# Where the norms, residuals and operand sums of a two-layer mixer block keep their intermediates: SBUF on two engines, or unused PSUM banks on VectorE alone

## The chip, the cores and the metric

The kernel runs on one core of a Trainium2 chip. The metric is device time in microseconds (us), from the start to the end of one execution. Five engines work beside each other and are kept in step by semaphores: TensorE (PE; PEld is its weight load), VectorE (DVE), ScalarE (ACT), GpSimd (POOL) and SyncE (SP), which here issues nearly all DMAs. Tensors lie in SBUF or in one of eight PSUM banks of 128 partitions x 512 float32 numbers; TensorE writes to PSUM.

## The reference, cut to what matters

Two layers over 256 context tokens and 1024 latent tokens of 1024 channels, in float32. Each layer normalises, projects, runs three recurrent mixers (retention, GLA, RWKV-7), projects back with `w_out`, adds a normed residual, normalises again, runs a SwiGLU of 2816 hidden channels, and adds a second normed residual:

```
def _rmsnorm(x, g, eps=1e-6):
    y = x * rsqrt(mean(x * x, axis=-1) + eps)
    return y * g

u = (rmsnorm(x) * (1 + sc1) + sh1) @ w_in
...
x = x + gt1 * rmsnorm(y @ w_out, norm_mix_post)
h = rmsnorm(x, norm_ffn_pre) * (1 + sc2) + sh2
f = (silu(h @ w_gate) * (h @ w_up)) @ w_down
x = x + gt2 * rmsnorm(f, norm_ffn_post)
```

The context tokens go through the same in the first layer alone.

## The kernel before, in words

Activations are held channel-major: 128 partitions by 8 channel tiles (`KT`, index kt) by the tokens of a block. There are three blocks: block 0 is the context (256 tokens), blocks 1 and 2 are 512 latent tokens each. A matmul keeps float32 accuracy by splitting both operands into a rounded high part and a low part (high on ACT by a cast, low by a subtraction), and making three products (`mm3`, `dense_cm`). Weights are split as they stream in: in `slot` (line 1459) ACT writes `shi` and POOL, for most slots, `slo` (L1464); in `weights` ACT writes `whi` and POOL `wlo` (L447).

Four helpers stand around the changed lines.

- `rstd` (L349) sums the squares of the 8 channel tiles over partitions by a matmul with ones into a bank of tag n (`pn`), and makes 1/sqrt(mean + eps) of it with Ln and Exp on ACT, in an SBUF tile `nrs`. With `pe=True` there is one ones-matmul for each kt. With `pe=False` ACT squares into `nacc`, `nacc2` and `nsq`, DVE adds the even kt (L370), POOL the odd ones (L372), DVE joins the two sums (L373), and one matmul follows.
- `resid` (L401) computes f = f * rstd * gain + x: the product into an SBUF tile `nv` of two buffers (L411: kt 2 and 5 on POOL, the other six on DVE), then a scalar_tensor_tensor on DVE (L412); the result goes to DRAM in two halves.
- `norm_here` (L392) multiplies in place (L398: kt 2 and 5 on POOL) and applies scale and shift on ACT.
- `split_norm` (L378) multiplies into `nv` (L386, same sharing), applies scale and shift on ACT, casts to the high part `xh` on DVE (L388), and subtracts to the low part `xl` (L390, odd kt on POOL, even kt on DVE).

`operands` (L1494) makes the sums and splits of a Strassen-like product for the hidden layer: s1 = a21 + a22, s2 = s1 - a11, s3 = a11 - a21 (L1510 to L1512) in the SBUF tiles `nsq`, `nacc` and `nacc2` of one buffer each, a21 = a12 - s2 (L1513), then a cast on ACT and a subtraction for S2, S3, S1 and 12 (L1503; S1 on POOL, the others on DVE).

The stretches of the program in which these run, in order:

- the start: `split_norm` of all three blocks, with `pe=True`, while the first `w_in` weights arrive; PSUM holds 3 banks of tag d (`pd`), 3 of tag m (`pm`), 2 of tag n. After it `rwkv_in` projects from `xh`, `xl` into `pd`.
- the FFN of the first layer (`ffn`, L1623), with 4 banks d, 3 banks m, 1 bank n: residual and norm of block 0 behind the last `w_out` column; then `hidden_plain` of block 0 (11 steps) on PE in banks d, with residual and norm of blocks 1 and 2 and `operands` issued between its steps; then `hidden` with the Strassen products. In this up part nothing uses the m banks.
- its down projection: a first pass over the weights for block 1, a second one for blocks 0 and 2. Products go through the m banks and DVE adds each to `facc` (L1741); the d banks are unused. Residual and `split_norm` of block 1 (`pe=False`) run under the second pass; those of blocks 0 and 2 (`pe=True`) follow it, and behind them the next layer's `rwkv_in`, for which both PSUM pools are closed and opened anew.
- the FFN of the second layer: the same without the context, residual, norm and `operands` of block 2 beside `hidden` of block 1 for three steps; at the very end the residual of block 2, which writes the output.

Instructions are put in order for each engine by a scheduler that simulates the time line; within an engine they run in that order. SP issues DMAs in the same way.

Of the kernel before, what the change touches and what calls it, by code (L numbers as in the profile page):

```python
# [50 lines left out]
NV = 2  # L51
# [120 lines left out]
class Kern:  # L172
# [176 lines left out]
    def rstd(self, x, b, dst, pe=False):  # L349


        nc = self.nc
        n = BLK[b][1]
        ps = self.pn()
        if pe:
            for kt in range(KT):
                sq = self.t(self.N, [128, 512], ("nsq", "nacc", "nacc2")[kt % 3], bufs=1)[:, :n]
                self.act(sq, x[:, kt, :], AF.Square)
                self.mm(ps[:, :n], self.ones, sq, start=kt == 0, stop=kt == KT - 1)
        else:  # L360
            acc = self.t(self.N, [128, 512], "nacc", bufs=1)[:, :n]
            acc2 = self.t(self.N, [128, 512], "nacc2", bufs=1)[:, :n]
            for kt in range(KT):
                if kt < 2:
                    self.act(acc2 if kt else acc, x[:, kt, :], AF.Square)
                    continue
                sq = self.t(self.N, [128, 512], "nsq", bufs=1)[:, :n]
                self.act(sq, x[:, kt, :], AF.Square)
                if kt % 2 == 0:
                    nc.vector.tensor_tensor(acc, acc, sq, op=ALU.add)  # L370
                else:
                    nc.gpsimd.tensor_tensor(acc2, acc2, sq, op=ALU.add)  # L372
            nc.vector.tensor_tensor(acc, acc, acc2, op=ALU.add)  # L373
            self.mm(ps[:, :n], self.ones, acc)
        self.act(dst, ps[:, :n], AF.Ln, bias="e6", scale=1.0 / D)
        self.act(dst, dst, AF.Exp, scale=-0.5)

    def split_norm(self, x, b, A, B, s, xh, xl, pe=False):  # L378

        nc = self.nc  # L380
        n = BLK[b][1]
        rs = self.t(self.N, [128, 512], "nrs", bufs=1)[:, :n]
        self.rstd(x, b, rs, pe)
        for kt in range(KT):
            v = self.t(self.N, [128, 512], "nv", bufs=NV)[:, :n]
            (nc.gpsimd if kt % 3 == 2 else nc.vector).tensor_tensor(v, x[:, kt, :], rs, op=ALU.mult)  # L386
            self.act(v, v, AF.Identity, bias=B[:, kt, s:s + 1], scale=A[:, kt, s:s + 1])
            nc.vector.tensor_copy(xh[:, kt, :], v)  # L388
            e = nc.gpsimd if kt % 2 else nc.vector
            e.tensor_tensor(xl[:, kt, :], v, xh[:, kt, :].bitcast(F32), op=ALU.subtract)  # L390

    def norm_here(self, x, b, A, B, s):  # L392

        n = BLK[b][1]
        rs = self.t(self.N, [128, 512], "nrs", bufs=1)[:, :n]
        self.rstd(x, b, rs)
        for kt in range(KT):
            (self.nc.gpsimd if kt % 3 == 2 else self.nc.vector).tensor_tensor(x[:, kt, :], x[:, kt, :], rs, op=ALU.mult)  # L398
            self.act(x[:, kt, :], x[:, kt, :], AF.Identity, bias=B[:, kt, s:s + 1], scale=A[:, kt, s:s + 1])

    def resid(self, f, b, gp, s, xsrc, xdst, pe=False, px=None):  # L401
# [5 lines left out]
        rs = self.t(self.N, [128, 512], "nrs", bufs=1)[:, :n]  # L407
        self.rstd(f, b, rs, pe)
# [1085 lines left out]
    def operands(self, xc, p, T):  # L1494
# [12 lines left out]
        for kt in range(4):  # L1507
            a11, a12, a21, a22 = T[0][:, kt, :], T[0][:, kt + 4, :], T[1][:, kt, :], T[1][:, kt + 4, :]
            s1, s2, s3 = (self.t(self.N, [128, 512], x, bufs=1)[:, :n] for x in ("nsq", "nacc", "nacc2"))
# [4 lines left out]
            for i, (name, src) in enumerate((("S2", s2), ("S3", s3), ("S1", s1), ("12", a12))):  # L1514
                split(name, kt, src, g if i % 3 == 2 else v)
# [452 lines left out]
```

## Time and profile before, and how to read it

| | |
|---|---|
| median of 3 runs | 4202.64 us (4200.39 to 4202.81) |
| the profiled execution | 4200.48 us, span 4198.7 us |
| PE busy | 3837.7 us (91%), 30414 instructions |
| PEld busy | 3170.7 us (76%) |
| DVE busy | 2668.9 us (64%), 4510 instructions |
| ACT busy | 1740.9 us (41%) |
| POOL busy | 1678.4 us (40%) |
| mean granted clock of PE | 0.951 |

The profile is one execution. A row of the windows view gives, for a stretch, its length and the busy time of each engine (with the number of instructions), the granted clock of TensorE as a share of full speed (1.00 is 2.4 GHz), the share of the DMA engines' time and the bytes moved. A row of the lines view gives a line of the program, engine, operation, output and inputs, shape, count, then busy us in total and mean ns of one, then the idle time of the engine before them and who ended it. A row of the waits view reads "engine line waited for: us in total, times, longest".

### The profile page before, as it was taken

The numbers are of one execution on the slowest core, as the hardware profiler recorded it, in microseconds if no ns is written. First come the engines' busy times: TensorE is split into PE (matmuls) and PEld (weight loads), VectorE is DVE, ScalarE is ACT, GpSimd is POOL, SyncE is SP. The second block draws the span as 40 slices with busy tenths as digits, with TensorE's granted clock in tenths as the row PEclk, the third lists the DMA queues.
The fourth block names the chain that finished last, engine by engine and source line by source line (L and its number), as shares of the span: only waits on it lengthen the run. The fifth ranks groups of instructions, "written<-read, shape, count | busy, mean of one in ns | idle before, by whom it ended". The sixth has DMA issues, their size and how long they took to land. (4 is left out here: it accounts for less than half of the span.)

```text
span 4198.7 us, 78278 instructions
## 1 busy us (share of the span) xinstructions
PE 3837.7 (91%) x30414; PEld 3170.7 (76%) x30414; DVE 2668.9 (64%) x4510; ACT 1740.9 (41%) x3490; POOL 1678.4 (40%) x1775
## 2 busy tenths in 40 slices
PE   6998999789988899999997997999889887999998
PEld 3777887776667888887785676888856667999876
DVE  3465657667647766665765464667667578556665
ACT  4443334244435644433423443343244355344432
POOL 3146630333338832224533245740433454222453
PEclk8998999999999899999998997999989889999999
DMA  5587545666433422225331387655673132212542
GB/s 174 137 229 192 142 130 151 186 188 192 141 122 126 151 103 80 81 90 192 132 106 55 86 232 198 137 140 141 206 225 117 57 126 89 86 71 95 185 163 95
DMA packets 624771, 582.55 MB, mean 139 GB/s; under 512 B 315276, under 2 KB 517264, under 8 KB 607504
## 3 DMA queue, kind: packets, MB, share of 16 engines
q1 hardware_dynamic: 624112, 576.50, 45.0%
q8 instruction: 240, 3.93, 0.4%
q0 software_dynamic: 288, 1.05, 0.1%
q14 instruction: 131, 1.07, 0.1%
HBM read 431.14 MB, written 146.28 MB: 138 GB/s over the span
## 5 line engine op out<-in xcount | busy, mean ns | idle before, releaser
L1464 POOL TENSOR_TENSOR slo<-raw,shi 128x512 fp32r<-128x512 f32 x467 | 690.9, 1494 | 964.6 <-ACT shi L1463 894.0
L1463 ACT CAST shi<-raw 128x512 fp32r<-128x512 f32 x478 | 293.0, 619 | 492.7 <-PE pd L246 196.3
L1741 DVE TENSOR_TENSOR f<-pm,f 128x512 f32<-128x512 f32 (+1 forms) x400 | 252.1, 635 | 186.7 <-PE pm L246 184.5
L246 PE MATMUL pm<-hh,shi 128*128 128x512 f32 (+1 forms) x880 | 333.8, 380 | 19.5 <-DVE f L1741 10.2
L246 PE MATMUL pm<-hl,shi 128*128 128x512 f32 (+1 forms) x880 | 327.2, 372 | 0.0
L246 PE MATMUL pm<-hh,slo 128*128 128x512 f32 (+1 forms) x880 | 326.3, 371 | 0.0
L447 POOL TENSOR_TENSOR wlo<-wraw,whi 128x512 fp32r<-128x512 f32 x120 | 166.8, 1399 | 386.7 <-ACT whi L446 376.1
L246 PE MATMUL pd<-whi,xh 128*128 128x256 f32 x1072 | 315.6, 296 | 1.9 <-DVE st L451 1.9
L246 PE MATMUL pd<-wlo,xh 128*128 128x256 f32 x1072 | 314.5, 294 | 1.8 <-POOL wlo L447 1.8
L246 PE MATMUL pd<-whi,xl 128*128 128x256 f32 x1072 | 315.0, 294 | 0.0
L246 PE MATMUL pd<-xl,whi 128*128 128x512 f32 (+1 forms) x720 | 278.1, 387 | 12.5 <-POOL xl L390 8.6
L246 PE MATMUL pd<-xh,whi 128*128 128x512 f32 (+1 forms) x720 | 276.9, 385 | 11.6 <-DVE xh L388 11.5
L246 PE MATMUL pd<-xh,wlo 128*128 128x512 f32 (+1 forms) x720 | 271.5, 377 | 1.1 <-POOL wlo L447 1.1
L1463 ACT CAST shi<-tw 128x512 fp32r<-128x512 f32 x200 | 123.6, 619 | 305.3 <-PE pd L246 231.9
L246 PEld LDWEIGHTS pd<-wlo,xh 128*128 128x128 f32 x1072 | 211.5, 197 | 10.3 <-issue 6.0
L246 PEld LDWEIGHTS pd<-whi,xh 128*128 128x128 f32 x1072 | 210.9, 197 | 9.2 <-DVE st L451 2.5
L246 PEld LDWEIGHTS pd<-whi,xl 128*128 128x128 f32 x1072 | 211.2, 197 | 5.8 <-issue 3.7
L246 PEld LDWEIGHTS pm<-hh,shi 128*128 128x128 f32 x880 | 167.5, 191 | 58.0 <-DVE f L1741 18.3
L246 PEld LDWEIGHTS pm<-hl,shi 128*128 128x128 f32 x880 | 167.8, 191 | 29.6 <-issue 1.7
L246 PEld LDWEIGHTS pm<-hh,slo 128*128 128x128 f32 x880 | 167.2, 190 | 28.9
L1464 DVE TENSOR_TENSOR slo<-tw,shi 128x512 fp32r<-128x512 f32 x200 | 145.1, 727 | 67.0 <-ACT shi L1463 66.7
L246 PEld LDWEIGHTS pd<-xl,whi 128*128 128x128 f32 x720 | 141.5, 197 | 53.3 <-POOL xl L390 13.5
(395 smaller groups left out, 11218.4 us busy)
## 6 DMA issues: line engine op xcount, KB each, us to landing
raw<-in_wgu SPq DMA_DIRECT2D x72, 1024.0 KB
wmod<-in_w_mod SPq DMA_DIRECT2D x192, 256.0 KB
raw<-in_wd SPq DMA_DIRECT2D x44, 1024.0 KB
wraw<-in_w_in SPq DMA_DIRECT2D x100, 256.0 KB
a<-ops SPq DMA_DIRECT2D x80, 288.0 KB
h<-h SPq DMA_DIRECT2D x44, 512.0 KB
h<-u SPq DMA_DIRECT2D x19, 1024.0 KB
X<-ops SPq DMA_DIRECT2D x36, 480.0 KB
```

The source lines that it names most:

```text
L246: return self.nc.tensor.matmul(out, l, r, start=start, stop=stop, skip_group_check=skip)
L447: nc.gpsimd.tensor_tensor(wl[i][:, :, w], r, wh[i][:, :, w].bitcast(F32), op=ALU.subtract)
L1463: self.nc.scalar.copy(hi, src)
L1464: e.tensor_tensor(lo, src, hi.bitcast(F32), op=ALU.subtract)
L1741: nc.vector.tensor_tensor(facc[b][:, m, :], ps, facc[b][:, m, :], op=ALU.add)
```

## The change

All intermediates of these helpers go to PSUM banks that the stretch doesn't use: `self.tmp` is `pm` (3 banks) at the start and in the up part, `pd` (4 banks) in the down part. `rstd` keeps 1/sqrt in its n bank, in place, and returns it, so the bank is held until the last product that reads it. With `pe=False` all seven sums go to DVE. The products of `resid`, `norm_here` and `split_norm` all go to DVE, with a PSUM output; scale and shift run from PSUM (in `split_norm` to PSUM). The high part of `split_norm` moves from DVE to ACT, and all low parts to DVE. In `operands` s1 to s3 lie in PSUM, S1 moves from POOL to DVE, and 12 from DVE to POOL. The tiles `nrs` and `nv` go away. In the down part `resid` and `split_norm` of blocks 0 and 2 change from `pe=True` to `pe=False`; at the start `pe=True` stays.

```diff
-    def rstd(self, x, b, dst, pe=False):
+    def rstd(self, x, b, pe=False):
...
+        acc = None if pe else self.tmp()[:, :n]
+        for kt in range(KT):
+            sq = self.t(self.N, [128, 512], ("nsq", "nacc", "nacc2")[kt % 3], bufs=1)[:, :n]
+            if not pe and kt == 0:
+                self.act(acc, x[:, kt, :], AF.Square)
+                continue
+            self.act(sq, x[:, kt, :], AF.Square)
+            if pe:
+                if kt == 0:
+                    ps = self.pn()[:, :n]
+                self.mm(ps, self.ones, sq, start=kt == 0, stop=kt == KT - 1)
+            else:
+                nc.vector.tensor_tensor(sq if kt == KT - 1 else acc, acc, sq, op=ALU.add)
+        if not pe:
+            ps = self.pn()[:, :n]
+            self.mm(ps, self.ones, sq)
+        self.act(ps, ps, AF.Ln, bias="e6", scale=1.0 / D)
+        self.act(ps, ps, AF.Exp, scale=-0.5)
+        return ps
...
     def split_norm(self, x, b, A, B, s, xh, xl, pe=False):
...
-            v = self.t(self.N, [128, 512], "nv", bufs=NV)[:, :n]
-            (nc.gpsimd if kt % 3 == 2 else nc.vector).tensor_tensor(v, x[:, kt, :], rs, op=ALU.mult)
+            v = self.tmp()[:, :n]
+            nc.vector.tensor_tensor(v, x[:, kt, :], rs, op=ALU.mult)
             self.act(v, v, AF.Identity, bias=B[:, kt, s:s + 1], scale=A[:, kt, s:s + 1])
-            nc.vector.tensor_copy(xh[:, kt, :], v)
-            e = nc.gpsimd if kt % 2 else nc.vector
-            e.tensor_tensor(xl[:, kt, :], v, xh[:, kt, :].bitcast(F32), op=ALU.subtract)
+            nc.scalar.copy(xh[:, kt, :], v)
+            nc.vector.tensor_tensor(xl[:, kt, :], v, xh[:, kt, :].bitcast(F32), op=ALU.subtract)
...
     def norm_here(self, x, b, A, B, s):
...
-            (self.nc.gpsimd if kt % 3 == 2 else self.nc.vector).tensor_tensor(x[:, kt, :], x[:, kt, :], rs, op=ALU.mult)
-            self.act(x[:, kt, :], x[:, kt, :], AF.Identity, bias=B[:, kt, s:s + 1], scale=A[:, kt, s:s + 1])
+            v = self.tmp()[:, :n]
+            self.nc.vector.tensor_tensor(v, x[:, kt, :], rs, op=ALU.mult)
+            self.act(x[:, kt, :], v, AF.Identity, bias=B[:, kt, s:s + 1], scale=A[:, kt, s:s + 1])
...
     def resid(self, f, b, gp, s, xsrc, xdst, pe=False, px=None):
...
-            v = self.t(self.N, [128, 512], "nv", bufs=NV)[:, :n]
-            (nc.gpsimd if kt % 3 == 2 else nc.vector).tensor_tensor(v, f[:, kt, :], rs, op=ALU.mult)
+            v = self.tmp()[:, :n]
+            nc.vector.tensor_tensor(v, f[:, kt, :], rs, op=ALU.mult)
             nc.vector.scalar_tensor_tensor(f[:, kt, :], v, gp[:, kt, s:s + 1], xo[:, kt, :], op0=ALU.mult, op1=ALU.add)
...
     def operands(self, xc, p, T):
...
-            s1, s2, s3 = (self.t(self.N, [128, 512], x, bufs=1)[:, :n] for x in ("nsq", "nacc", "nacc2"))
+            split("12", kt, a12, g)
+            s1, s2, s3 = (self.tmp()[:, :n] for _ in range(3))
...
-            for i, (name, src) in enumerate((("S2", s2), ("S3", s3), ("S1", s1), ("12", a12))):
-                split(name, kt, src, g if i % 3 == 2 else v)
+            for name, src in (("S2", s2), ("S3", s3), ("S1", s1)):
+                split(name, kt, src, v)
...
     def ffn(self, l, f, gp1, A2, B2, gp2, A1n, B1n):
...
+        self.tmp = self.pm
...
+        self.tmp = self.pd
...
-                self.resid(facc[b], b, gp2, s, self.XD[1], self.out if last else self.XD[0], b != 1)
+                self.resid(facc[b], b, gp2, s, self.XD[1], self.out if last else self.XD[0])
...
-                    self.split_norm(facc[b], b, A1n, B1n, s, nh[b], nl[b], b != 1)
+                    self.split_norm(facc[b], b, A1n, B1n, s, nh[b], nl[b])
...
     def run(self):
...
+        self.tmp = self.pm
```

## Rows read from the trace of the kernel before

**Rows 1.** The windows view: the eight stretches in which the changed helpers run.

```profile
38.00:97.00 59.00, 42.66 (x108) 22.07 (x107) 36.43 (x54) 33.74 (x56) 31.31 (x40) 0.75 0.23 63
1236.00:1255.00 19.00, 1.73 (x7) 0.94 (x6) 9.60 (x20) 7.15 (x17) 9.18 (x10) 0.64 1.04 392
1255.00:1481.00 226.00, 190.95 (x1217) 172.71 (x1216) 165.59 (x154) 136.28 (x249) 186.45 (x128) 0.90 0.42 146
2040.00:2120.00 80.00, 71.77 (x374) 59.01 (x373) 66.92 (x95) 34.05 (x57) 39.92 (x28) 0.96 0.32 110
2238.00:2306.00 68.00, 45.53 (x127) 25.86 (x126) 39.12 (x65) 32.84 (x58) 27.73 (x37) 0.80 0.29 85
3434.00:3541.00 107.00, 80.57 (x553) 75.39 (x553) 103.05 (x149) 59.72 (x112) 52.02 (x33) 0.90 0.26 94
4060.00:4090.00 30.00, 27.87 (x116) 21.20 (x115) 27.65 (x36) 10.24 (x15) 18.89 (x12) 1.00 0.49 173
4177.00:4199.00 22.00, 3.40 (x8) 1.14 (x6) 11.70 (x15) 1.95 (x3) 3.28 (x2) 0.65 0.26 96
```

**Rows 2.** Single lines: count, then shortest, median and longest duration in ns.

```profile
L1741 DVE TENSOR_TENSOR f<-pm,f x400: 408/691/693, 1926.6 to 4177.0; 128x512 f32<-128x512 f32 x108, 128x256 f32<-128x256 f32 x26
L412 DVE SCALAR_TENSOR_TENSOR f<-nv,gain,xl x80: 472/742/1786, 1243.3 to 4192.1; 128x512 f32<-128x512 f32 x64, 128x256 f32<-128x256 f32 x16
L398 DVE TENSOR_TENSOR f<-f,nrs x30: 411/1472/1784, 1264.0 to 3506.3; 128x512 f32<-128x512 f32 x24, 128x256 f32<-128x256 f32 x6
L1464 POOL TENSOR_TENSOR slo<-raw,shi x467: 1255/1297/3213, 925.0 to 4163.6; 128x512 fp32r<-128x512 f32 x156
```

**Rows 3.** The time line of DVE near 4070 us: start, length, times.

```profile
4070.40 1.27 DVE L1741 TENSOR_TENSOR f<-pm,f 128x512 f32<-128x512 f32 x2
```

**Rows 4.** The lines view of DVE and POOL, 1255 to 1481 us.

```profile
L412 DVE SCALAR_TENSOR_TENSOR f<-nv,gain,xl 128x512 f32<-128x512 f32 x16 | 21.4, 1359 | 0.1
L398 DVE TENSOR_TENSOR f<-f,nrs 128x512 f32<-128x512 f32 x12 | 19.5, 1690 | 0.1
L372 POOL TENSOR_TENSOR nacc<-nacc,nsq 128x512 f32<-128x512 f32 x12 | 19.0, 1587 | 4.8 <-ACT nsq L239 4.8
```

**Rows 5.** The waits of PE, 1255 to 1481 us.

```profile
PE pd L246 <- DVE u L1618: 13.3, 3, 5.9
PE pd L246 <- POOL slo L1464: 9.0, 10, 3.0
```

**Rows 6.** The lines view of DVE and POOL, 3434 to 3541 us.

```profile
L1464 DVE TENSOR_TENSOR slo<-tw,shi 128x512 fp32r<-128x512 f32 x23 | 20.6, 910 | 0.1
L412 DVE SCALAR_TENSOR_TENSOR f<-nv,gain,xl 128x512 f32<-128x512 f32 x8 | 9.8, 1236 | 0.0
L1503 POOL TENSOR_TENSOR S1l<-nsq,S1h 128x256 fp32r<-128x256 f32 x4 | 9.0, 2252 | 7.7 <-ACT S1h L1502 7.7
```

**Rows 7.** The waits of PE, 2040 to 2120 us.

```profile
PE pm L246 <- DVE f L1741: 8.2, 11, 2.0
```

**Rows 8.** The lines view of ACT, whole span.

```profile
L239 ACT ACTIVATE nv<-nv,modT,gain 128x512 f32<-128x512 f32 x32 | 25.4, 811 | 35.0 <-DVE nv L386 30.7 <-POOL nv L386 4.2
L1463 ACT CAST shi<-raw 128x512 fp32r<-128x512 f32 x478 | 293.0, 619 | 492.7 <-PE pd L246 196.3 <-PE pm L246 130.2 <-issue 120.3
```

**Rows 9.** The time line of DVE at the start: the last `split_norm`, first and last of 17 pieces.

```profile
76.41 1.69 DVE L386 TENSOR_TENSOR nv<-f,nrs 128x512 f32<-128x512 f32 x2 [0.81 <-ACT nrs L239]
...
92.90 0.47 DVE L388 CAST xh<-nv 128x512 fp32r<-128x512 f32 x1 [0.94 <-ACT nv L239]
```

**Rows 10.** The windows view of PE's instructions on tile pd alone, before `rwkv_in` runs freely.

```profile
2238.00:2286.00 48.00, 10.61 (x48) 0.89 0.36 104
```

**Rows 11.** The time lines of PE and DVE in the last 22 us.

```profile
4176.80 1.88 PE L246 MATMUL pn<-nacc,ones 128*128 128x512 f32 x4
...
4181.81 1.29 DVE L411 TENSOR_TENSOR nv<-f,nrs 128x512 f32<-128x512 f32 x2 [4.12 <-ACT nrs L239]
...
4191.49 1.40 DVE L412 SCALAR_TENSOR_TENSOR f<-nv,gain,xl 128x512 f32<-128x512 f32 x2
```

More of the change, by code (lines that the diff above doesn't have):

```diff
@@ L50 @@
 C2 = 1
-NV = 2
 PA = 7
@@ L346, in mod_gain @@
         return o
-    def rstd(self, x, b, dst, pe=False):
+    def rstd(self, x, b, pe=False):
         nc = self.nc
         n = BLK[b][1]
[L354 to L376, printed above, removed]
+        acc = None if pe else self.tmp()[:, :n]
[17 more added lines that the diff above has]
+        return ps
     def split_norm(self, x, b, A, B, s, xh, xl, pe=False):
@@ L381, in split_norm @@
         n = BLK[b][1]
-        rs = self.t(self.N, [128, 512], "nrs", bufs=1)[:, :n]
-        self.rstd(x, b, rs, pe)
+        rs = self.rstd(x, b, pe)
         for kt in range(KT):
-            v = self.t(self.N, [128, 512], "nv", bufs=NV)[:, :n]
-            (nc.gpsimd if kt % 3 == 2 else nc.vector).tensor_tensor(v, x[:, kt, :], rs, op=ALU.mult)
+            v = self.tmp()[:, :n]
+            nc.vector.tensor_tensor(v, x[:, kt, :], rs, op=ALU.mult)
             self.act(v, v, AF.Identity, bias=B[:, kt, s:s + 1], scale=A[:, kt, s:s + 1])
-            nc.vector.tensor_copy(xh[:, kt, :], v)
-            e = nc.gpsimd if kt % 2 else nc.vector
-            e.tensor_tensor(xl[:, kt, :], v, xh[:, kt, :].bitcast(F32), op=ALU.subtract)
+            nc.scalar.copy(xh[:, kt, :], v)
+            nc.vector.tensor_tensor(xl[:, kt, :], v, xh[:, kt, :].bitcast(F32), op=ALU.subtract)
     def norm_here(self, x, b, A, B, s):
         n = BLK[b][1]
-        rs = self.t(self.N, [128, 512], "nrs", bufs=1)[:, :n]
-        self.rstd(x, b, rs)
+        rs = self.rstd(x, b)
         for kt in range(KT):
-            (self.nc.gpsimd if kt % 3 == 2 else self.nc.vector).tensor_tensor(x[:, kt, :], x[:, kt, :], rs, op=ALU.mult)
-            self.act(x[:, kt, :], x[:, kt, :], AF.Identity, bias=B[:, kt, s:s + 1], scale=A[:, kt, s:s + 1])
+            v = self.tmp()[:, :n]
+            self.nc.vector.tensor_tensor(v, x[:, kt, :], rs, op=ALU.mult)
+            self.act(x[:, kt, :], v, AF.Identity, bias=B[:, kt, s:s + 1], scale=A[:, kt, s:s + 1])
     def resid(self, f, b, gp, s, xsrc, xdst, pe=False, px=None):
@@ L406, in resid @@
         self.dma(xo, xsrc[:, :, t0:t0 + n])
-        rs = self.t(self.N, [128, 512], "nrs", bufs=1)[:, :n]
-        self.rstd(f, b, rs, pe)
+        rs = self.rstd(f, b, pe)
         for kt in range(KT):
-            v = self.t(self.N, [128, 512], "nv", bufs=NV)[:, :n]
-            (nc.gpsimd if kt % 3 == 2 else nc.vector).tensor_tensor(v, f[:, kt, :], rs, op=ALU.mult)
+            v = self.tmp()[:, :n]
+            nc.vector.tensor_tensor(v, f[:, kt, :], rs, op=ALU.mult)
             nc.vector.scalar_tensor_tensor(f[:, kt, :], v, gp[:, kt, s:s + 1], xo[:, kt, :], op0=ALU.mult, op1=ALU.add)
```

## The prediction, made before the changed kernel was run

> **What bounds the kernel now.** I read the page first: PE is busy for 91% of the span, so a step off another engine is worth only what it gives back to PE. Then I cut out the eight stretches in which the changed helpers run, with the windows view [rows 1]. Together they are 611 us long, and PE is busy for 464 of them: 147 us idle, and a granted clock between 0.64 and 1.00 where the kernel's mean is 0.951. Everything the change can win is there. They differ in what fills them: from 1255 to 1481 us POOL works for 186 of 226 us and DVE for 166; from 3434 to 3541 us DVE works for 103 of 107; at the start and from 2238 to 2306 us no engine is full, and a chain from engine to engine sets the pace.
>
> Third, single lines. A DVE addition of a PSUM bank to an SBUF tile (L1741) has a median of 0.691 us and a longest of 0.693 in 400 instances, though POOL splits weights beside it. The same size with all tensors in SBUF starts from the same length and stretches to 1.79 us (L412), and for L398 the median is 1.47 us. POOL's weight split stretches too, from 1.26 to 3.21 us [rows 2]. So in this trace DVE and POOL hold each other up when both read SBUF for two inputs, and a DVE instruction with one input in PSUM is out of it. The changed instructions are nearly all of the held-up kind, and they become the other kind.
>
> **Price of an instruction after the change.** Two L1741 in a row take 1.27 us [rows 3], 0.64 each; I take 0.62 for 512 columns in a full queue and 0.35 for 256. No row shows DVE writing to PSUM. The nearest rows read PSUM and write SBUF [rows 2], and I take their price; from below I allow 0.58, since nothing excludes a small gain, from above 0.72, a tenth of a us more. For ACT I take 0.81 for scale and shift and 0.62 for a cast [rows 8], as from SBUF. The Trainium skill, page "ScalarE: Activation LUTs", in the walk through an activation, says that an ACT result in PSUM is quicker than one in SBUF; no row shows it, and by it the two stretches in which ACT sets the pace would end slightly earlier still.
>
> **The sum, stretch by stretch** (negative is time saved).
>
> *The start, 38 to 97 us.* The last `split_norm` takes from 76.41 to 93.4 us, 17 us [rows 9], with two `nv` buffers going round DVE, POOL and ACT. After: 16 DVE instructions of 0.62 are 10 us, ACT's 8 x (0.81 + 0.62) are 11.4, and three banks keep them overlapped, so some 13 us: 4 saved in each of the two wide blocks. Against it, ACT gets 8 casts of 0.4 and 16 of 0.62 more, 13 us on top of its 33.7 in 59 [rows 1]. I take -7, between -12 (59 less ACT's 47) and +2.
>
> *Behind `w_out`, 1236 to 1255 us.* PE idles 17 of 19 us [rows 1] while the first two rstd are made in a chain. A POOL sum of each stands in one queue with weight splits of at least 1.26 us [rows 2]; on DVE it doesn't. The DMA is full there (share 1.04 [rows 1]), so what follows may be late anyway: -3, from -5 to 0.
>
> *`hidden_plain` of block 0, 1255 to 1481 us.* DVE: the 16 L412 fall from 21.4 to 9.9 us; the 12 wide L398 take 19.5 [rows 4], and their 16 successors take 9.9. The other products and sums go the same way, less the four products and twelve sums that arrive from POOL: altogether about 45 us less on DVE. POOL loses 12 sums (19.0 us [rows 4]), 8 wide products and two narrow ones, and the four S1, gains four 12, and its 88 weight splits no longer stretch: about 54 us less. PE's idle time is 35 us, of which the waits for L1618, which stands in DVE's queue, and for POOL's `slo` are 13.3 and 9.0 [rows 5]; and the clock of 0.90 costs 22 us more. I give back two thirds of those 22 us of waits and some of the rest, -18 in all, and 8 of the 22 us of clock: -26, from -45 to -10.
>
> *Block 1 under the second down pass, 2040 to 2120 us.* PE waits 8.2 us for L1741, in 11 waits [rows 7], behind norm instructions in DVE's queue. DVE's part in the norm shrinks by about 9 us of 67, casts and stretching included: -5, from -8 to 0. From 4060 to 4090 us, the residual alone, PE idles 2.1 us [rows 1]: -1.
>
> *Between the layers, 2238 to 2306 us.* Here I put gains against losses. Two `split_norm` shorten as at the start: about -3 (narrow) and -4.5 (wide). Some six narrow ones-matmuls leave the stream of products, at half or less of the 0.94 us that a wide one takes [rows 11]: -2. But the seven sums of each norm, and the four products that POOL did, now stand in DVE's chain: +4.5. And there is a new wait: the d banks, free before, are now `tmp`, and `rwkv_in` writes to d banks. In the trace PE does 10.6 us of that projection before 2286 us, while the last block is still being normed [rows 10]. That work will wait until the last products have left the banks. It is queued in front of everything PE does next; half of it still overlaps the last `split_norm`: +5. Net 0, from -9 to +9.
>
> *`hidden` of block 1 beside block 2, 3434 to 3541 us.* DVE is full, so each us taken from it counts. L412 falls from 9.8 to 5.0 us; the products save 2; the sums cost 2 more; splits from PSUM save 2; the others balance: -8. POOL's 52 us lose some 23, the four S1 of 2.25 us each among them [rows 6], so that what stays in SBUF on DVE is held up less (the 23 `slo` at 0.910 us lie 0.3 above their unhindered length): -7. Together -15, from -26 (all of PE's idle time) to -5.
>
> *The end, 4177 to 4199 us.* The last four ones-matmuls run one after the other behind the last product (1.88 us for the first two, in four records [rows 11]) and leave PE's stream: -3.5 together, one DVE sum more included. Then 16 DVE instructions without POOL take 10.4 us, where they and POOL's two took from 4181.8 to 4192.9, 11.1 us [rows 11]: -0.5. I take -4, from -5 to 0.
>
> The sum is -7 - 3 - 26 - 5 - 1 + 0 - 15 - 4 = -61. The profiled execution took 4200.5 us by itself, so 4139.5; the median of the runs is 2.2 us higher, and I forecast **4141 us**.
>
> **The rivals.**
>
> *Only the edges go* (4180 us). The 226 us from 1255 on hold 22 us of waits with names of DVE and POOL; if the chain ACT `shi`, `slo`, PE sets the pace there, freeing DVE only moves the wait to ACT, whose queue gets nothing lighter. Then that stretch gives 5 instead of 26 and the DVE-full one 5 instead of 15, and the start 2 instead of 7, together -25 with the small ones: 4178, say 4180. For it: PE's longest waits are few. Against: POOL is busy 82% there.
>
> *All the idle time comes back* (4091 us): the lower ends of all terms add to -112, less 2 for the median. For it: the clock falls only where PE idled, so one us saved brings more.
>
> *A write to PSUM costs DVE more than one to SBUF* (4233 us, slower). There are 312 of them: 18 norms of 6 sums and 8 products each, 3 of 8 products at the start, 36 operand sums. Nearly all lie in the eight stretches. At 0.3 us more each, 94 us against 61 saved: +33. It decides from 0.2 us each, which is 61 through 312. Against it: the reads of PSUM cost 0.69 like the unhindered ones of SBUF [rows 2]. The Trainium skill, page "VectorE: DVE Perf Modes", section Specifications, puts VectorE closer to SBUF and ScalarE closer to PSUM; by that such a write would be the slow kind, and it gives no figure. No row here shows it, hence a small chance.
>
> *The change does little* (4200 us): the new wait on the d banks costs all of the 10.6 us, ACT with 13 us more at the start gives nothing back, and the order that the scheduler makes elsewhere loses what is left.
>
> **How the numbers follow.** Forecast 0.50; edges only 0.25, of which a quarter ends within 0.2% of before; all of it 0.12; little 0.07; slow writes 0.06. A measurement of this kernel can tell 0.2%, 8.4 us, from no change. Faster by more than that: 0.50 + 0.19 + 0.12 = 0.81. Within: 0.06 + 0.07 = 0.13; I leave 0.12 and give 0.07 to slower, for the d banks may cost more than I said. The range goes from 4095, just inside the full recovery, to 4188, which takes in the edges-only case and leaves out the last two: 4095 to 4188.
>
> **What would show it right or wrong.** After the change, L412, and the products of L411, L386 and L398, should have medians near 0.69 us and longest lengths below 0.8; POOL's `slo` should have a median nearer to its shortest, 1.26 us. The stretch from 1255 us should be some 26 us shorter with a clock above 0.93, the DVE-full one 15 us shorter. The projection between the layers should start late, with PE idle until the last products. The forecast is wrong if the medians of DVE's writes to PSUM lie near 0.9 us or above; if the stretches with `hidden_plain` keep their length although DVE and POOL work less; or if ACT is found full at the start.

## The result and the profile after

The changed kernel takes 4101.64 us (median of four runs, 4095.16 to 4110.53) beside 4202.73 us for the kernel before on the same chip: ratio 0.9761, interval 0.9742 to 0.978, that is 101 us less. Run once more, beside experiments 3, 10 and 11, it gave 0.9754 (0.9735 to 0.9773). I forecast 4141, 61 us less, inside a range that holds the result. The direction and the mechanism are right; the size is short by 40 us, and the text below is about where those lie. The profiled execution of the changed kernel took 4102.32 us, its span 4100.5.

The windows view of the changed kernel, first over the stretches that answer to [rows 1] in the same order, then over one that [rows 1] did not have (3291 to 3359 us). Columns: stretch, length, busy time of PE, PEld, DVE, ACT, POOL, granted clock, DMA share, GB/s.

```profile
38.00:80.00 42.00, 34.60 (x106) 17.90 (x106) 25.70 (x46) 40.55 (x78) 10.35 (x22) 0.96 0.55 137
1227.00:1245.00 18.00, 3.55 (x12) 2.33 (x11) 12.41 (x31) 9.07 (x22) 3.40 (x4) 0.62 1.04 390
1245.00:1440.00 195.00, 186.44 (x1295) 170.52 (x1295) 133.62 (x193) 142.84 (x268) 144.37 (x110) 0.99 0.53 182
1982.00:2050.00 68.00, 66.25 (x367) 56.21 (x367) 56.09 (x96) 36.30 (x63) 20.23 (x16) 1.00 0.36 128
2166.00:2236.00 70.00, 14.52 (x45) 9.36 (x44) 45.62 (x88) 37.58 (x73) 10.12 (x21) 0.54 0.28 82
3359.00:3450.00 91.00, 76.35 (x545) 72.09 (x545) 90.81 (x155) 57.62 (x109) 33.42 (x24) 0.91 0.31 111
3968.00:3998.00 30.00, 28.57 (x123) 22.67 (x123) 24.29 (x35) 10.03 (x15) 12.74 (x10) 1.00 0.56 192
4079.00:4101.00 22.00, 1.90 (x6) 0.61 (x4) 12.88 (x21) 2.50 (x4) 0.00 (x0) 0.63 0.26 96
...
3291.00:3359.00 68.00, 57.65 (x248) 45.11 (x247) 50.91 (x89) 45.25 (x93) 30.22 (x25) 0.89 0.47 169
```

Read the third line first. Beside `hidden_plain` PE idled 35 of 226 us before [rows 1]; now it idles 8.6 of 195, at a clock of 0.99 instead of 0.90. POOL has 144 us of work there instead of 186. Line six: DVE is still full (90.8 of 91 us), the stretch 16 us shorter. Line one: ACT is now full, 40.6 of 42 us, and the stretch is shorter all the same. Line five, between the layers: PE does 14.5 us of work where it did 45.5, and the stretch is not shorter.

Single lines of the changed kernel, as in [rows 2]: count, then shortest, median, longest in ns, first and last start, forms. L365 is a sum of a norm, L391 and L403 products, L404 the residual addition, L1503, L1504 and L1505 the three operand sums, L1456 the weight split.

```profile
L365 DVE TENSOR_TENSOR pm<-pm,nacc x40: 419/688/700, 1228.3 to 3404.3; 128x512 f32<-128x512 f32 x32, 128x256 f32<-128x256 f32 x8
...
L391 DVE TENSOR_TENSOR pm<-f,pn x40: 414/683/697, 1245.8 to 3423.4; 128x512 f32<-128x512 f32 x32, 128x256 f32<-128x256 f32 x8
...
L403 DVE TENSOR_TENSOR pm<-f,pn x40: 416/684/697, 1234.0 to 3391.3; 128x512 f32<-128x512 f32 x32, 128x256 f32<-128x256 f32 x8
...
L404 DVE SCALAR_TENSOR_TENSOR f<-pm,gain,xl x40: 472/739/750, 1235.0 to 3394.7; 128x512 f32<-128x512 f32 x32, 128x256 f32<-128x256 f32 x8
...
L1503 DVE TENSOR_TENSOR pm<-f x12: 419/817/1782, 1364.9 to 3449.2; 128x256 f32<-128x256 f32 x8, 128x512 f32<-128x512 f32 x4
...
L1504 DVE TENSOR_TENSOR pm<-pm,f x12: 414/420/700, 1366.3 to 3450.2; 128x256 f32<-128x256 f32 x8, 128x512 f32<-128x512 f32 x4
...
L1505 DVE TENSOR_TENSOR pm<-f,f x4: 680/684/1649, 1367.5 to 1387.0; 128x512 f32<-128x512 f32 x4
...
L1456 POOL TENSOR_TENSOR slo<-raw,shi x467: 1252/1297/3215, 914.9 to 4070.0; 128x512 fp32r<-128x512 f32 x156
```

A DVE write into PSUM costs what a write into SBUF costs, 0.69 us at 512 columns, and no product, sum or residual addition is longer than 0.75. The exceptions are L1503 and L1505: they write PSUM, but both inputs are SBUF, and they still go to 1.78 and 1.65 us. L1504, between them, has one input in PSUM and ends at 0.70. That suggests which operand matters; two runs below test it.

PE's waits in the changed kernel over 1245 to 1440 us, 1982 to 2050 us and 2166 to 2236 us (total us, times, longest), against [rows 5] and [rows 7]:

```profile
PE pd L245 <- POOL slo L1456: 5.9, 7, 1.3
PE pd L245 <- DVE u L1611: 1.7, 1, 1.7
...
PE pd L245 <- ACT shi L1455: 0.2, 1, 0.2
...
PE pm L245 <- DVE f L1736: 0.9, 1, 0.9
...
PE pn L245 <- DVE nacc L365: 43.4, 3, 16.8
PE pd L245 <- DVE xl L383: 12.0, 1, 12.0
```

The 13.3 us of waits for DVE's `u` are down to 1.7, the 8.2 for `facc` to 0.9. New are 43.4 us in which PE waits between the layers for sums of squares, with nothing else that it may start; what they cost is taken up under experiment 5.

**Where the time went**, from landmarks that all kernels have (the last `u` copy of `rwkv_in`, the last copy of a `w_out` bank, the first Strassen `s` copy, the first `facc` copy, the last `facc` addition, the last `gyt` copy): length of each stretch before, and by how much it changed. Each column is one profiled execution.

```
stretch up to                     before  forecast  after  again  all_in  operands  scale_in  scale_alone  banks
                                                                  _sbuf   _as_bef.  _sbuf     _in_psum     _swapped
last u copy, layer 1               307.7    -7      -16.6  -15.1  -12.4   -17.5     -12.2      -2.1        -14.6
last w_out copy (mixers)           928.5     0       +8.0   +9.9   -5.2    +3.7      +1.5      +4.1         +2.7
first s copy (hidden_plain)        252.9   -29      -40.8  -40.3   -5.8   -23.1     -25.3      -8.7        -39.4
first facc copy (Strassen)         425.9     0       -7.9   -7.6   +0.1    -6.0      -7.1      -4.8         -6.1
last facc addition (down)          323.5    -5      -14.2  -14.2   -9.6   -14.6      -9.0      -7.0        -18.2
last u copy, layer 2               262.0     0      +11.1  +10.8   +2.4   +12.3     +13.6      +6.8         +4.1
last gyt copy (mixers)             853.1     0       -1.9   -1.5   +5.2    -2.4      -3.2      -4.4         -5.1
first s copy (w_out, norms)         80.2     0      -13.1  -13.1   -7.6   -11.1      -8.5      -4.9        -10.9
first facc copy                    497.4   -15      -16.9  -18.3   -5.6   -10.5     -11.0      -5.4        -15.4
last facc addition (down)          245.8    -4.5     -4.9   -4.4   -0.9    -4.7      -4.2      +0.2         -7.3
end                                 21.7    -0.5     -1.1   -0.1   -1.3    -1.0      -1.0      -0.5         -1.5
```

The column "again" is the same kernel a second time: it repeats to within 1.5 us in every row but one, the first mixers, where it differs by 1.9. The kernel of the last column issues the same instructions in the same order on TensorE up to the first down pass, and there differs by up to 7 us: the mixers' rows scatter that much, the others can be read.

### The profile page after: what moved, and what is told of

It reads as the page before. It is cut to its first block, busy times and chain, and to the rows that moved or that the text cites. A ratio compares the mean times of both kernels' runs of the same rounds, so it can differ in the third digit from the quotient of the medians.

```text
span 4100.5 us, 78165 instructions
## 1 busy us (share of the span) xinstructions
PE 3765.7 (92%) x30344; PEld 3125.4 (76%) x30344; DVE 2590.2 (63%) x4602; ACT 1755.4 (43%) x3538; POOL 1507.7 (37%) x1670
## 5 line engine op out<-in xcount | busy, mean ns | idle before, releaser
L1456 POOL TENSOR_TENSOR slo<-raw,shi 128x512 fp32r<-128x512 f32 x467 | 668.2, 1446 | 1084.0 <-ACT shi L1455 996.4
L1456 DVE TENSOR_TENSOR slo<-tw,shi 128x512 fp32r<-128x512 f32 x200 | 143.5, 718 | 64.9 <-ACT shi L1455 64.8
L245 PEld LDWEIGHTS pd<-xh,whi 128*128 128x128 f32 x720 | 140.1, 195 | 49.1 <-DVE xl L383 13.5
```

What stands on the lines that cost most here:

```text
L245: return self.nc.tensor.matmul(out, l, r, start=start, stop=stop, skip_group_check=skip)
L1456: e.tensor_tensor(lo, src, hi.bitcast(F32), op=ALU.subtract)
```

## The experiments

**1. Everything back in SBUF, engines as after.** Is it where the operands lie, or which engine does the work?

```diff
-        self.tmp = self.pm          (and self.pd)
+        self.tmp = self.nv          # three SBUF buffers, tag "nv"
...
-        self.act(ps, ps, AF.Ln, ...); self.act(ps, ps, AF.Exp, ...); return ps
+        self.act(rs, ps, AF.Ln, ...); self.act(rs, rs, AF.Exp, ...); return rs
```

> The changed kernel with every instruction on the engine where the change put it, but with the intermediates back in SBUF: three buffers in place of the three or four PSUM banks, the scale of each norm in SBUF, two buffers for the squares instead of three so that it fits. Theory P (placement: an operand in PSUM takes DVE out of the hold-up with POOL): the products, sums and splits on DVE stretch again from 0.69 us to 1.2 us and more, and since DVE now has all of them, the stretch with hidden_plain comes back to 220 us or more; 4190 to 4230 us in all. Theory E (engines: what counted was that the norms' steps no longer stand behind weight splits in POOL's queue): most of the gain stays, 4100 to 4125 us. Half way (about 4150) would give each half.

Measured: 0.9918 (0.9894 to 0.9943), 34 us faster than before instead of 101 to 103. So neither theory alone: two thirds of the gain are the place. One third stays with everything in SBUF: the engines, and with them a third `nv` buffer where the kernel before had two, which no run separates (this kernel also has one square buffer less than after the change, and three intermediates instead of four in the down pass). The table says which third: the start, the down pass of the first layer and half of the norms before the last `s` copy keep most of their gain, `hidden_plain` nearly nothing. Lines and windows of this kernel (products, residual addition, weight split; then the `hidden_plain` stretch):

```profile
L395 DVE TENSOR_TENSOR nv<-f,nrs x40: 411/680/1789, 1234.0 to 3473.0; 128x512 f32<-128x512 f32 x32, 128x256 f32<-128x256 f32 x8
...
L408 DVE SCALAR_TENSOR_TENSOR f<-nv,gain,xl x80: 474/743/1792, 1223.1 to 4151.8; 128x512 f32<-128x512 f32 x64, 128x256 f32<-128x256 f32 x16
...
L1460 POOL TENSOR_TENSOR slo<-raw,shi x467: 1256/1301/8932, 912.1 to 4127.8; 128x512 fp32r<-128x512 f32 x156
...
1246.00:1472.00 226.00, 186.64 (x1262) 171.78 (x1261) 164.09 (x185) 138.93 (x255) 157.85 (x104) 0.92 0.43 148
```

DVE's work beside `hidden_plain` is back at 164 us (133.6 after the change, 165.6 before), the clock at 0.92, and one weight split of POOL is held for 8.9 us.

**2. Only the scale back in SBUF; results stay in PSUM.** Which operand counts?

```diff
+        rs = self.t(self.N, [128, 512], "nrs", bufs=1)[:, :n]
-        self.act(ps, ps, AF.Ln, ...); self.act(ps, ps, AF.Exp, ...); return ps
+        self.act(rs, ps, AF.Ln, ...); self.act(rs, rs, AF.Exp, ...); return rs
```

> The changed kernel with one thing moved: the scale of each norm lies in SBUF again, so the products read two SBUF tensors and write a PSUM bank; sums, residual additions and splits still have an input in PSUM. Theory In (what takes DVE out of the hold-up is an input in PSUM, not the output): the products' medians stay near 0.68 us but their longest go to 1.7 us or more; beside hidden_plain 48 of them lose some 0.25 us each, 12 us of DVE's time, and in the DVE-full stretch 4 to 6: 4110 to 4125 us. Theory Out (a write to PSUM is enough): longest below 0.8 us, 4098 to 4106 us.

Measured: 0.9833 (0.9817 to 0.985), 30 to 33 us of the gain gone, more than I expected, and the products' median rose too, to 1.20 us, where I had 0.68. Products (two SBUF inputs, PSUM output) and residual additions (one PSUM input):

```profile
L392 DVE TENSOR_TENSOR pm<-f,nrs x40: 419/1198/1798, 1243.8 to 3455.7; 128x512 f32<-128x512 f32 x32, 128x256 f32<-128x256 f32 x8
...
L405 DVE SCALAR_TENSOR_TENSOR f<-pm,gain,xl x40: 471/734/741, 1233.0 to 3420.9; 128x512 f32<-128x512 f32 x32, 128x256 f32<-128x256 f32 x8
```

So here writing into PSUM protects nothing; reading from it does.

**3. The reverse: the kernel before, only the scale in PSUM**, and with it two of every eight products moved to DVE, which POOL made before.

```diff
-        self.act(dst, ps[:, :n], AF.Ln, ...); self.act(dst, dst, AF.Exp, ...)
+        self.act(ps, ps, AF.Ln, ...); self.act(ps, ps, AF.Exp, ...); return ps
...
-            (nc.gpsimd if kt % 3 == 2 else nc.vector).tensor_tensor(v, f[:, kt, :], rs, op=ALU.mult)
+            nc.vector.tensor_tensor(v, f[:, kt, :], rs, op=ALU.mult)          (in all three helpers)
```

> The kernel before with one thing moved: the scale of each norm stays in the PSUM bank that the ones-matmul filled, and all products are made by DVE from there (POOL made every third). Sums, the products' results, operand sums and split stay in SBUF and with POOL as before. Theory In (an input in PSUM is what counts, and parts add up): DVE's products keep below 0.8 us, and the 30 us that the changed kernel lost when its scale went back to SBUF are won here, 4165 to 4182 us. Rival (what remains in SBUF on DVE and POOL takes the hold-up over, so that a part by itself brings little): 4188 to 4205 us.

Measured: 0.9925 (0.9908 to 0.9941), 32 us. The products' output is in SBUF here, and L398 of this run is never longer than 0.69 us (before, its median was 1.47 [rows 2]), while the residual addition with all tensors in SBUF keeps its 1.78:

```profile
L398 DVE TENSOR_TENSOR f<-f,pn x40: 405/674/689, 1263.8 to 3481.4; 128x512 f32<-128x512 f32 x32, 128x256 f32<-128x256 f32 x8
...
L411 DVE SCALAR_TENSOR_TENSOR f<-nv,gain,xl x80: 470/744/1784, 1245.3 to 4164.9; 128x512 f32<-128x512 f32 x64, 128x256 f32<-128x256 f32 x16
```

Theory In holds from both sides, and the scale is worth about as much alone (32, POOL's share of the products included) as inside the full change (30 to 33). The Trainium skill, page "SBUF — State Buffer", section "Who interferes with whom", says this in general: a DVE instruction with two SBUF inputs contends with a GpSimd instruction that reads SBUF, one with at most one SBUF input, outside the modes that use both of DVE's ports, does not. L391, L392 and L398 above agree with it in both directions.

**4. The operand sums as before, the norms changed.**

```diff
-            split("12", kt, a12, g)
-            s1, s2, s3 = (self.tmp()[:, :n] for _ in range(3))
+            s1, s2, s3 = (self.t(self.N, [128, 512], x, bufs=1)[:, :n] for x in ("nsq", "nacc", "nacc2"))
...
-            for name, src in (("S2", s2), ("S3", s3), ("S1", s1)):
-                split(name, kt, src, v)
+            for i, (name, src) in enumerate((("S2", s2), ("S3", s3), ("S1", s1), ("12", a12))):
+                split(name, kt, src, g if i % 3 == 2 else v)
```

> The changed kernel with the operand sums undone: s1, s2, s3 in SBUF, S1 split on POOL, 12 on DVE, as before the change; the norms stay changed. Theory P: the stretch in which DVE is full (before w_out's second half of the last layer) gets back the greater part of the 30 us that it lost, 12 to 20 us, and the stretch with hidden_plain 5 to 10 us more: 4118 to 4132 us. Rival (the norms carry the gain, operand sums are a small part): 4102 to 4110 us.

Measured: 0.982 (0.9797 to 0.9842), 25 to 28 us given back, the sum that theory P expected, but shared out the other way: 18 beside `hidden_plain` (-23.1 against -40.8), 8 in the two stretches around the last `s` copy.

**5. The sums of squares of the down pass by TensorE again.**

```diff
-                self.resid(facc[b], b, gp2, s, self.XD[1], self.out if last else self.XD[0])
+                self.resid(facc[b], b, gp2, s, self.XD[1], self.out if last else self.XD[0], b != 1)
...
-                    self.split_norm(facc[b], b, A1n, B1n, s, nh[b], nl[b])
+                    self.split_norm(facc[b], b, A1n, B1n, s, nh[b], nl[b], b != 1)
```

> The changed kernel with the sums of squares of the down pass made by TensorE's ones-matmuls again where they were (blocks 0 and 2). By the prediction's terms they cost 3.5 us at the end and 2 between the layers, against a DVE chain of 4.5 us that they spare between the layers: 4101 to 4106 us. Rival (the between-layer chain on DVE is the dearer part, since the first u copy of layer 1 came 1.4 us later in its stretch than before and the last 11 later): faster, 4090 to 4098 us. In both cases the end from the last facc addition on gets 0 to 4 us longer.

Measured: 0.9767 (0.9742 to 0.9792): no difference that can be told. In the trace, the two down passes are 2.9 and 3.7 us longer than after the change (-11.3 and -1.2 in the rows where it had -14.2 and -4.9), and the stretch between the layers is the same (+11.2). The forecast's 3.5 and 2 are there; the rival, that the DVE chain is the dearer part, has nothing in its row, and neither has the 4.5 us that I had booked for that chain. PE's waits between the layers show why: in this run (2166 to 2240 us) the ones-matmuls wait for products of the norm before, and in the kernel before (2238 to 2306 us) they waited for ACT's squares, at most 3.7 us at a time:

```profile
PE pn L245 <- DVE pd L403: 14.4, 2, 9.0
...
PE pn L245 <- DVE pd L380: 7.9, 1, 7.9
```

```profile
PE pn L246 <- ACT nsq L239: 7.0, 3, 3.7
```

The scale lies in the only n bank until the last product has read it, and the next norm's ones-matmuls write that bank. So with the scale in PSUM, TensorE can no longer sum one norm's squares under the products of the norm before, and it gains nothing over DVE here. Experiment 3 has the same wait for its products L410 (2220 to 2291 us), and is 6.8 us longer in this row though its projection starts as early as before:

```profile
PE pn L246 <- DVE nv L410: 18.1, 2, 10.3
```

In the profiled execution of experiment 5 the second mixers were 13 us shorter than after the change, which hid the loss; I can't explain those.

**6. The banks of the down pass exchanged.**

```diff
-        self.tmp = self.pd
...
-                            ps = self.pm()[:, :n]
+                            ps = self.pd()[:, :n]
```

> The changed kernel with the banks of the down pass exchanged: the products accumulate in the four d banks, the intermediates lie in the three m banks, so that rwkv_in of the second layer finds the d banks free as soon as the last products are added. The prediction's new wait (10.6 us of projection that cannot start, priced at 5): the projection starts some 20 us after the last product instead of 61, the first u copy of layer 1 comes 5 to 10 us earlier, 4092 to 4098 us. Rival (the projection is queued behind the last split_norm anyway, or the mixers give it back): 4100 to 4104 us. One bank less for the intermediates could cost up to 3 us, one more for the products gains at most their waits, 1 us.

Measured: 0.9739 (0.9716 to 0.9762). `rwkv_in` of the second layer starts 17 us after the last product instead of 62, as the matmuls of its projection show, from the last `facc` addition to 2236 us, of the changed kernel and of this one (count; first and last start):

```profile
L245 PE MATMUL pd<-xh,whi x11: 397/415/628, 2228.7 to 2235.7; 128*128 128x256 f32 x8, 128*128 128x512 f32 x3
```

```profile
L245 PE MATMUL pd<-xh,whi x43: 280/389/793, 2179.8 to 2235.6; 128*128 128x512 f32 x27, 128*128 128x256 f32 x16
```

The row up to the last `u` copy goes from +11.1 to +4.1. So the new wait costs 7 us, at the last `u` copy: 5 of them come before the first `u` copy, which follows the last addition by 61.7 instead of 67.0 us, and behind it PE idles 6.7 of 204 us, for a reason that isn't known. The kernel with all intermediates in SBUF, which has no such wait, shows +2.4 in that row. A second effect was not expected: with four banks for the products PE idles 0.0 instead of 1.8 us from the last `facc` copy to the last addition, and the row of the down pass is 4 us shorter (2 of them idle time, the rest busy time, which I can't explain).

**7. Only the start changed.** The kernel before, with the new `split_norm` in its first three calls.

```diff
-            self.split_norm(f[b], b, A1, B1, 1 if b == 0 else 0, xh[b], xl[b], True)
+            self.split_norm0(f[b], b, A1, B1, 1 if b == 0 else 0, xh[b], xl[b])     # products, scale/shift in m banks, cast on ACT
```

> The kernel before with the new split_norm at the start alone (three calls); all else, the other norms and the operands, as before. The stretch up to the first u copy of the first layer should be 14 us shorter, as in the changed kernel. Theory Kept: those 14 us reach the end, 4180 to 4188 us. Theory Given back (the mixers of the first layer lost 7 to 8 of the gain on the way in the changed kernel, so it is their order or their DMA that gives it back): 4188 to 4195 us.

Measured: 0.9964 (0.9951 to 0.9977), 15 us; in the trace 14.1 at the last `u` copy and 10.9 at the end. Between the two theories, nearer to Kept: the first mixers took 1.9 of it and the stretch with `hidden_plain` 1.8. What the mixers of the first layer take in the changed kernel (+8.0, +9.9) is within their own scatter, since the other kernels with the same start show +1.6 to +9.1.

**8. Half of the start's casts on DVE**, with the exchanged banks.

```diff
-            nc.scalar.copy(xh[:, kt, :], v)
+            (nc.vector.tensor_copy if pe and kt % 2 else nc.scalar.copy)(xh[:, kt, :], v)
```

> The changed kernel with exchanged banks (as banks_swapped) and, in the three norms of the start, every second cast on DVE instead of ACT: 12 casts, some 6 us, leave ACT, which is busy 40.6 of 42 us there, and go to DVE, which is busy 25.7. If ACT sets the pace of the start, the first u copy of the first layer comes 4 to 6 us earlier and 3 to 6 of it reach the end: 4083 to 4087 us. If another link of the chain sets it, nothing: 4087 to 4092 us.

Measured: 0.9724 (0.971 to 0.9739), the lowest of all, though its interval still touches that of the changed kernel's second measurement. From 38 to 79 us ACT is busy 36.0 of 41 us and DVE 32.0, but the first `u` copy comes only 1 us earlier than with the exchanged banks alone (77.7 against 78.6) and the last 4.6 earlier, and the mixers' scatter hides what became of these. ACT was full, yet not the only link: with some 4 us less on it the start moved by 1.

**9. The weight differences of the Strassen products in the m banks**, with the exchanged banks.

```diff
-            t = self.t(W, [128, 512], "tw", bufs=3)
+            t = self.pm()
```

> The changed kernel with exchanged banks (as banks_swapped) and the weight differences of the Strassen products (tw, three SBUF buffers) in the three m banks, which are idle there. Theory P carried on: the splits of tw on DVE and the second differences lose their stretched cases (longest 1.78 us, now below 0.8); in the DVE-full stretch that is some 3 to 5 us, elsewhere PE is busy 98% and nothing is to be won: 4083 to 4087 us. Rival (the operand sums of block 2 want the same three banks, and the ring holds one up for the other): 4090 us or more.

Measured: 0.9733 (0.9712 to 0.9753), as the exchanged banks alone. Two effects cancel. The Strassen row of the first layer goes from -6.1 to -12.7. And in the last layer the row up to the first `facc` copy goes from -15.4 to +0.9, while the one before it, up to the first `s` copy, goes from -10.9 to -17.9: together 9 us lost, as the rival said: the differences share three banks with the norm and operand sums of block 2, and PE waits (3339 to 3450 us):

```profile
PE pd L245 <- ACT shi L1455: 18.9, 2, 14.7
PE pn L245 <- DVE nacc L365: 16.7, 1, 16.7
```

**10 and 11. The differences in the m banks only where no norm runs; and some splits back on POOL.**

```diff
+        self.mfree = l < DEPTH - 1 or j >= J1
...
-            t = self.t(W, [128, 512], "tw", bufs=3)
+            t = self.pm() if self.mfree else self.t(W, [128, 512], "tw", bufs=3)
...
-                self.nc.vector.tensor_tensor(lo[:, kt, :], x, h[:, kt, :].bitcast(F32), op=ALU.subtract)
+                (g if g and kt % 2 else self.nc.vector).tensor_tensor(...)      (in the second of the two alone)
```

> The changed kernel with exchanged banks (as banks_swapped) and the weight differences of the Strassen products in the m banks only where no norm or operand sum uses them: all of the first layer, and the second from its fourth pair on. The run with all of them there won 6.5 us in the products of the first layer and lost 16 in the DVE-full stretch to the shared ring. If both readings hold, 0.968 to 0.972 of the kernel before (4076 to 4086 us at its usual 4202); if the 6.5 us were scatter, as banks_swapped, 0.972 to 0.975.

> As swapped_free_diffs, and every second of the splits of operands 22 and S4 in the last layer on POOL, which is busy 36 of 104 us in the DVE-full stretch where DVE is busy 100. If DVE's queue sets the pace there, 3 to 5 us less than swapped_free_diffs; if these splits, two SBUF inputs on either engine, hold POOL and DVE up again, the same or up to 5 us more.

Measured: 0.9737 (0.9719 to 0.9756) and 0.9751 (0.9722 to 0.9779). The first misses its forecast; the second lands where its rival had it, no faster than the first, with runs from 4079 to 4116 us. The Strassen row of the first layer is at -12.8 and -12.9, so those 6.5 us were no scatter; but in the last layer the rows up to the first `s` copy and up to the first `facc` copy, together -26.3 with the exchanged banks alone, are at -20.9 and -20.5, and the second mixers are 7 and 12 us longer. Which of these is the banks' doing isn't settled.

**12. The changed kernel again**, beside experiments 3, 10 and 11.

> The changed kernel itself, unaltered, once more, for the comparison with the runs beside it on the same chip: a ratio of 0.974 to 0.978 to the kernel before.

Measured: 0.9754 (0.9735 to 0.9773).

No version clearly beats the changed kernel. Those with exchanged banks lie at 0.9724 to 0.9751 against 0.9754 to 0.9761; the 7 us between the layers are plain in each trace, a total of that size is at the limit of these intervals.

## Why the prediction was right, and where it was too small

**Price of a write to PSUM: right.** 0.68 to 0.69 us as median at 512 columns, and at the end four in a row take 2.49 us, 0.60 from one start to the next, where I took 0.62. The slow-write rival falls: the DVE lines above are its test. (Its 4233 leaves out the 2 us that the forecast adds for the median; nothing hangs on it.) The rule that puts VectorE closer to SBUF has no cost here. The Trainium skill, page "ScalarE: Activation LUTs", section "Step-by-step: what each stage is for", also has ACT quicker into PSUM than into SBUF; the trace agrees in direction. Scale and shift went from 811 ns [rows 8] to 780 and 758 with source and result in PSUM, and to 788 in `norm_here`, whose result lies in SBUF, so that some 10 to 30 ns are left for the result:

```profile
L238 ACT ACTIVATE pm<-pm,modT,gain 128x512 f32<-128x512 f32 x16 | 12.3, 780 | 0.8 <-DVE pm L380 0.8
L238 ACT ACTIVATE pd<-pd,modT,gain 128x512 f32<-128x512 f32 x16 | 11.7, 758 | 2.4 <-DVE pd L380 2.4
...
L238 ACT ACTIVATE f<-pm,modT,gain 128x512 f32<-128x512 f32 x32 | 24.3, 788 | 0.7 <-DVE pm L391 0.7
```

In `split_norm` that is 2 us over 48 instructions, the 16 narrow ones included, nothing that decides.

**The mechanism: right, and now sharper.** "A DVE instruction with one input in PSUM is out of it" was read from L1741; experiments 2 and 3 show that it is the input, not the output, and experiment 1 prices the place at 67 us of 101. POOL gains too, as forecast: beside `hidden_plain` the median of its splits went from 1704 to 1297 ns:

```profile
L1464 POOL TENSOR_TENSOR slo<-raw,shi x88: 1255/1704/2416, 1266.4 to 1480.0; 128x512 fp32r<-128x512 f32 x88
```

```profile
L1456 POOL TENSOR_TENSOR slo<-raw,shi x92: 1262/1297/1835, 1252.6 to 1439.9; 128x512 fp32r<-128x512 f32 x92
```

**The start, -7: measured -15 to -17, so the term was less than half its size.** I counted what the last `split_norm` would save in each wide block. ACT waited in all three, 18.8 us in all, for products, which I read as standing in line for two `nv` buffers (no run changes the number of buffers alone); the first line is the kernel before from 38 to 93 us, the second the changed one from 38 to 79:

```profile
L239 ACT ACTIVATE nv<-nv,modT,gain 128x512 f32<-128x512 f32 (+1 forms) x24 | 17.4, 739 | 18.8 <-DVE nv L386 16.8 <-POOL nv L386 2.0
```

```profile
L238 ACT ACTIVATE pm<-pm,modT,gain 128x512 f32<-128x512 f32 (+1 forms) x24 | 16.6, 705 | 0.8 <-DVE pm L380 0.8
```

The casts, some 12 us on ACT, went into that idle time. ACT was found full at the start, which I had named as a sign against the forecast. It wasn't one: a full engine at the end of a shorter stretch is where the gain stops, not a loss. Three quarters of it are not the place at all: with everything in SBUF and three buffers the start still gains 12.4 of 16.6; engines and buffers are not told apart there.

**Behind `w_out` and `hidden_plain`, -29: measured -41, and -8 more in the Strassen products behind it.** The step that failed is "two thirds of those 22 us of waits and some of the rest, and 8 of the 22 us of clock". The windows view from the last `w_out` copy to the first `s` copy, of the kernel before and of the changed one:

```profile
1236.00:1489.00 253.00, 200.69 (x1276) 181.14 (x1276) 182.68 (x183) 148.35 (x275) 198.94 (x139) 0.89 0.47 168
```

```profile
1228.00:1440.00 212.00, 189.38 (x1300) 172.44 (x1301) 146.03 (x224) 151.56 (x289) 146.77 (x112) 0.96 0.57 199
```

PE's idle time fell from 52 to 23 us, by 30 where I had 21 with the 3 behind `w_out`, and its busy time by 11, as the clock rose from 0.89 to 0.96, where I had 8. DVE's work fell by 37 us, where I had 45, POOL's by 52, where I had 54. I had counted on the waits that carry a name of DVE or POOL; what came back is nearly all of PE's idle time beside `hidden_plain` (35 to 8.6 us), whatever name it had. My window also ended 8 us before the last of it. The "only the edges go" rival falls with this row: PE waits 0.2 us for ACT's `shi` there now (5.5 before), so the wait did not move on to it.

**Block 1 under the down pass, -5: measured -14.** The waits for `facc` went as forecast, 8.2 to 0.9. Not in the term: the clock, 0.96 to 1.00 [rows 1], and some 3 us of ones-matmuls that I had booked between the layers.

**Between the layers, 0 from -9 to +9: measured +11, outside its bounds.** The new wait was seen, and taken at 5 instead of 7. The norms gave nothing, though the two `split_norm` did shorten, from first product to last low part: by 5.9 us (narrow, 14.2 to 8.3) and 6.6 (wide, 18.4 to 11.8), where I had 3 and 4.5. What ate this are the gaps in which the next 1/sqrt is made, in front of the products of narrow `split_norm`, wide `resid` and wide `split_norm`: 5.3, 2.3 and 3.6 us before, 8.0, 8.1 and 8.8 now, 14 more, where I had 4.5 for the longer chain. The sums on DVE alone are not to blame, for with TensorE's sums (experiment 5) the gaps are 8.5, 7.4 and 8.8, there because the ones-matmuls must wait for the n bank that holds the scale, a cost that my sum did not have. So the first `u` copy comes 1.3 us later in its stretch; the other 10 us come after it, when PE, busy 204.5 of 206 us, makes up the projection that it did meanwhile before.

**The DVE-full stretch, -15: measured -17.** Right. But "everything the change can win is there", said of the eight stretches, was wrong: a ninth, 3353 to 3434 us before (w_out of the last layer with the norms of block 1), gave 13 more. It holds products and sums of the same lines; I had cut the windows by idle PE and not by the first and last start of each changed line.

**The end, -4, and the residual alone, -1: measured -6 together** (the last two rows of the table). Right; experiment 5 shows the ones-matmuls at 3.7 of it.

Put together, the trace shows 98 us against my 61. Beyond the forecast lie 13 in the missed stretch, 12 with `hidden_plain`, 10 at the start, 9 in the down pass, 8 in the Strassen products and 5 in the smaller rows; 11 between the layers and 8 in the first mixers go the other way.

## What to carry to other kernels

Where DVE and POOL work side by side, look for DVE instructions whose two inputs are both SBUF, and move one input, not the output, to an idle PSUM bank: the scale of a norm, with its products all on DVE, gave 32 us. When such a change is priced, list the stretches by the first and last start of every changed line, and where the clock is down beside PE's waits, count on its coming back with them (0.90 to 0.99 here). Before idle banks are used as scratch, ask who opens them next: here the next layer's projection did, and it cost 7 us until the banks were exchanged. And ask who must wait while a bank is kept for what lies in it: here the next norm's sums of squares did.

## What was not expected of the hardware

The hold-up is not shared evenly. In experiment 1, from 3394 us on, DVE ran 18 short instructions in a row, all with two SBUF inputs, none stretched, and POOL's weight split that began at 3394.36 us lasted 8.9 us, seven times its length; the lines of DVE just behind its start and around its end:

```profile
3394.44 0.42 DVE L1507 TENSOR_TENSOR nv<-f 128x256 f32<-128x256 f32 x1
3394.78 0.42 DVE L1510 TENSOR_TENSOR f<-f,nv 128x256 f32<-128x256 f32 x1
3395.11 0.42 DVE L1499 TENSOR_TENSOR S2l<-nv,S2h 128x256 fp32r<-128x256 f32 x1
...
3402.07 0.43 DVE L1560 TENSOR_TENSOR u<-pd,s 128x256 f32<-128x256 f32 x1
3402.41 1.43 DVE L368 TENSOR_TENSOR nv<-nv,nacc 128x512 f32<-128x512 f32 x1
```

The split ended at 3403.29, 1.22 us after DVE began its first instruction with an input in PSUM (L1560), and that is about what an unhindered split takes (1.26); the DVE instruction behind it took 1.43 instead of 0.69. So this one case reads as if the split got its turn only there. Elsewhere it is DVE whose instruction goes to 1.79. So an engine can lose to several instructions of the other in a row, and moving more work of that kind to DVE can starve POOL. Beside `hidden_plain`, in the same run, one split took 7.2 and one 3.7 us; how much of what experiment 1 failed to gain there is theirs isn't shown. Lengths on POOL are rough in these profiles, but 8.9 us is far outside any of the changed kernel (longest 3.2).
